# Matrix product in Winograd form on one core: in the first region of a row group, T1 of B's blocks goes ahead of the quarter sums of S4, and three of those sums move into the room of S2

## The chip, the cores and the metric

The kernel runs on one core of a Trainium2 chip. The metric is device microseconds (us) of one execution, the median of several. TensorE (PE) multiplies, VectorE (DVE) makes sums and adds results up, ScalarE (ACT) copies PSUM banks out and squares blocks, GpSimd (POOL) and SyncE (SP) issue transfers (ACT issues a few too).

## The reference

```
x = np.matmul(a, b)                    # a, b: 4096 x 4096 float32
return np.where(x > 0, x, alpha * x)   # alpha = 0.01
```

The kernel computes it in float16 blocks by Winograd's form of Strassen's scheme (seven block products in place of eight). On the way it squares A and B and takes the sums' extremes, and a branch at the end falls back to a plain bfloat16 product when the inputs are too uneven. That fallback is not taken here.

## The kernel before

**Regions.** The output is cut into regions of 1024 x 1024. A region is a pair (g, j): row group g of four, column block j of four. After the first region, which is computed while the inputs arrive, the program walks through `regions`, one group after the other. In a region A has the blocks A11, A12, A21, A22 and B has B11, B12, B21, B22, where each block is 512 columns (or rows of the output) wide and 2048 deep, in two tiles k = 0, 1 of 1024.

**Products.** `PRODUCTS` (L652) lists the seven: A11 B11, A12 B21, S2 T2, S3 T3, S1 T1, A22 T4, S4 B22. `product(n, ...)` (L792) issues number n: 64 matmuls of 128x512 at L801. The sums of A are made once for a group (`sum_a`, L566). The sums of B are made in every region, in place, by `b_sum` (L586, seen in the profile as L588): T3 into the room of B12, T2 into the room of B11, T4 into the room of B21, and T1 = B22 - T2 over T2, in the room of B11. T1 therefore has to wait until product 2 (S2 T2) has read T2, and product 4 (S1 T1) has to wait for T1.

**Quarters.** In the regions of groups 1 to 3 other than the last of groups 1 and 2, products 5 (A22 T4) and 6 (S4 B22) are themselves done by the same scheme on quarters: `sixth_in_quarters` (L843) and `seventh_in_quarters` (L892), seven `quarter_product`s of 16 matmuls of 128x256 each (L751). These need the quarter sums of A22 and of S4, four tiles each of 128x2048 float16 (512 KB). `sums_of_a` (L692) makes them: `make` takes a room, does one DVE sum (L700) and has SP store the result to DRAM (L701: `kept_qs` for S4's, `kept_qa` for A22's), from where the later regions of the group load them again (L743). This happens in the first region of each of the groups 1, 2 and 3, which the trace shows from about 412, 787 and 1160 us. Those three regions are what the change touches.

**Rooms.** S4's four sums and three of A22's four come from `new_a16()` (L762), a pool of three tiles of 512 KB, handed out in turn. So S4's fourth sum takes the tile of S4's first and has to wait until that one's store has landed; A22's first three wait for the stores of S4's second, third and fourth. The fourth of A22 lies in `t[:, 3]`. `t` (L1100) is a tile of four such rooms that is allocated right after product 2, in the room that S2 leaves. Its first three rooms serve from L1134 on for the quarter sums of B, which `sums_of_b` (L681; L686, L688, L690) makes for the sixth product.

**Order.** The order on each engine is the order of the program text. On DVE, in the first region of a group: T3 and T2 (only in group 1; the others load them), S3 and S4, the adds of product 1 to the kept sum (L967) and its leaky form (L312), T4 (L588), S4's quarter sums (L700), T1 (L588), A22's quarter sums (L700), then `t3_of_b` and `sums_of_b` (L680 to L690), the sum of two kept results (`add_v`, L972), and the adds that empty the banks of the fifth and the sixth product (L967, L856).

On PE in the same region: products 0 to 4, then the sixth product's quarter products in this order, where each names what it needs or which bank it fills: A22's (0,0) into bank one; sum 1 of A22 times sum 1 of B into bank other; (0,1) into the fourth bank; sum 2 times sum 2 onto one; sum 4 onto other; sum 3 onto one; (1,1) into the third. A bank is used again only after DVE's L856 has read it.

POOL issues the next region's blocks of B (L532, two transfers of 512 KB for each tile) whenever a product has read the old ones. SP's queue carries the output stores (L978), the copy of S4's quarter (1, 0) to DRAM (L716) and the stores of L701.

Of the kernel before, what the change touches and what calls it, by code (L numbers as in the profile page):

```python
# [47 lines left out]
def kernel(  # L48
# [402 lines left out]
    for i in range(1, len(steps)):  # L451
        t, h, u, first, last = steps[i]
# [19 lines left out]
        t, h, u, first, last = steps[i]  # L472
# [202 lines left out]
    def quarters_of_a(g, name):  # L675
        return {(h, k): operand(g, name, k)[:, :, h * HALF:(h + 1) * HALF, :] for h in range(2) for k in range(2)}
# [15 lines left out]
    def sums_of_a(g, name, room):  # L692

        x = {key: q.rearrange("p c m e -> p c (m e)") for key, q in quarters_of_a(g, name).items()}
        made = {}

        def make(n, x0, x1, op):
            made[n] = room(n)
            f = lambda t: made[t].rearrange("p (c m) -> p c m", m=2 * HALF) if isinstance(t, int) else x[t]
            nc.vector.tensor_tensor(f(n), f(x0), f(x1), op)  # L700
            nc.sync.dma_start(kept_q[name][n - 1], made[n])  # L701

        make(1, (1, 0), (1, 1), ADD)
        make(2, 1, (0, 0), SUB)
        make(3, (0, 0), (1, 0), SUB)
        make(4, (0, 1), 2, SUB)

    def x21(g, name):
        return operand(g, name, 0)[:, :, HALF:, :]

    def by_chunk(t):
        return t.rearrange("p c m e -> p c (m e)") if len(t.shape) == 4 else t.rearrange("p (c m) -> p c m", m=2 * HALF)

    def keep_x21(g, name):
        if g < G - 1:
            nc.sync.dma_start(by_chunk(kept_x21[name]), by_chunk(x21(g, name)))  # L716
# [45 lines left out]
    def new_a16(_=None):  # L762
        return a16_pool.tile([P, QUARTER], DT, name="q16", tag="a16")
# [18 lines left out]
    for i, (g, j) in enumerate(regions):  # L782
# [210 lines left out]
        def fetch_a(h, half, n):  # L993
            if n == 0:
                coming["rows", h, half] = small_pool.tile([P, 16], FP32, name="rows", tag=f"rows{half}")
            coming[h, half][n][0]()
# [21 lines left out]
        first_of_group = i == 0 or regions[i - 1][0] != g  # L1018
# [17 lines left out]
        if have_t2:  # L1036
            for k in ks:
                t = have_b[i, k, 0] = b_pool.tile([P, KC, NT], DT, name="b", tag="b11")
# [46 lines left out]
        if turning and g:  # L1085
            t3_of_b(quarters_of_b(i, 0, 1))
            for n in range(3):
                fetch_a(0, 1, n)
        if first_of_group and g:
            keep_x21(g, "s4")  # L1090
            sums_of_a(g, "s4", new_a16)
        if not g:
            bring_a(0, 1)

# [4 lines left out]
        if g:  # L1099
            t = x_pool.tile([P, 4, QUARTER], DT, name="q", tag="x")  # L1100
# [9 lines left out]
        if late_ones:  # L1110
            late_ones[0].end()
        if in_quarters and first_of_group:
            sq = {4: t[:, 3]}
            sums_of_a(g, "a22", lambda n: sq.setdefault(n, sq[4] if n == 4 else new_a16()))
            keep_x21(g, "a22")
# [106 lines left out]
    with tc.If(even == 0):  # L1222
        for m in range(M // RM):
            a_blocks = []
            for u in range(KU):
                t = a_pool.tile([P, KC // 2, RM, 2], BF16, name="a", tag=f"a{u // 2 + 1}{m % 2 + 1}")
# [6 lines left out]
            for n in range(N // NT):  # L1233
                banks = [new_bank(n % 2 * 4 + mt) for mt in range(MT)]
                cols = slice(n * NT, (n + 1) * NT)
                for u in range(KU):
                    t = b_pool.tile([P, KC, NT], BF16, name="b", tag=f"b{u // 2 + 1}{n % 2 + 1}")
# [8 lines left out]
                for mt in range(MT):  # L1246
                    t = c_pool.tile([P, 2, NT], FP32, name="c", tag=f"c{side}")[:, 0]
# [44 lines left out]
```

## Time and profile before

| what | value |
|---|---|
| median of 3 runs | 1536.24 us (1536.0 to 1539.86) |
| profiled execution | 1538.0 us |
| its span, first to last instruction | 1535.8 us |
| granted TensorE clock | 0.999 |
| PE busy, matmuls | 1523.6 us, 99% |
| DVE busy | 1158.6 us, 75% |
| ACT busy | 426.2 us, 28% |
| POOL busy | 281.8 us, 18% |
| B's blocks by POOL (q0) | 129.00 MB in all, 52.7% of 16 DMA engines' span |
| SP's transfers (q1) | 186.81 MB, 33.1% |

PE is busy nearly without a break and at full clock, so a change of the time has to appear as idle time of PE that comes or goes. The DMA share of the page's second section is in its upper tenths for most of the span: transfers share the DMA engines with many others, and how long one takes depends on what else is under way.

### The profile page before, as it was taken

Reading aid. Unit: us, or ns where it says so; the run is one execution under the profiler, and the core shown is the slowest. Engines: PE = TensorE matmul, PEld = TensorE weight load, DVE = VectorE, ACT = ScalarE, POOL = GpSimd, SP = SyncE. Lnnn points to the kernel's source line nnn. Section 1 sums busy time; section 2 is a strip of 40 time slices with the busy share of each in tenths; the row PEclk is TensorE's granted clock in tenths of the full one; section 3 lists DMA queues with packets and bytes.
Section 4 is the critical chain, followed back from the end, with each engine's and each line's share of the span. In section 5 each row is a group of like instructions: output and inputs, shape, how many; then the busy total and the mean of one; then the engine's idle time right before and its main releaser. Section 6 shows DMA issues by size and latency. Waiting matters only on the chain. (4 is left out here: it accounts for less than half of the span.)

```text
span 1535.8 us, 21827 instructions
## 1 busy us (share of the span) xinstructions
PE 1523.6 (99%) x8667; PEld 846.6 (55%) x8667; DVE 1158.6 (75%) x1207; ACT 426.2 (28%) x730; POOL 281.8 (18%) x458
## 2 busy tenths in 40 slices
PE   9999999999999999999999999999999999999998
PEld 4444444444445567574544747557554475746656
DVE  4368867765698686768769798686976968788497
ACT  2201344646310312103551031312464103041220
POOL 5641110143202011022220201110331110101100
PEclk9999999999999999999999999999999999999999
DMA  9999895998879979599798989959899895948934
GB/s 243 186 215 205 235 279 172 180 194 174 226 281 276 259 171 273 135 290 263 163 269 276 289 190 204 277 148 327 169 231 286 238 280 143 275 169 193 279 128 140
DMA packets 205442, 342.87 MB, mean 223 GB/s; under 512 B 18833, under 2 KB 148113, under 8 KB 195346
## 3 DMA queue, kind: packets, MB, share of 16 engines
q0 software_dynamic: 136704, 129.00, 52.7%
q1 hardware_dynamic: 62002, 186.81, 33.1%
q10 hardware_dynamic: 6624, 25.56, 4.4%
q8 instruction: 70, 1.15, 0.3%
q14 instruction: 42, 0.34, 0.1%
HBM read 361.76 MB, written 106.43 MB: 305 GB/s over the span
## 5 line engine op out<-in xcount | busy, mean ns | idle before, releaser
L801 PE MATMUL ps<-b,a 128*128 128x512 f16 x2624 | 570.9, 379 | 0.1
L801 PE MATMUL ps<-b,s 128*128 128x512 f16 x2240 | 489.2, 379 | 1.0 <-ACT c L814 1.0
L801 PEld LDWEIGHTS <-a 128*128 128x128 f16 x2624 | 256.8, 98 | 308.1 <-issue 0.6
L801 PEld LDWEIGHTS <-s 128*128 128x128 f16 x2240 | 219.0, 98 | 263.8 <-DVE b L588 1.5
L588 DVE TENSOR_TENSOR b<-b 128x4096 f16<-128x4096 f16 x104 | 235.1, 2289 | 66.7 <-DMA b<-in_b_dram 62.1
L532 POOL DMA_DIRECT2D b<-in_b_dram x160 | 118.5, 746 | 862.2 <-PE ps L751 325.2
L814 ACT COPY c<-ps 128x512 f32<-128x512 f32 x164 | 84.6, 596 | 444.9 <-PE ps L801 401.1
L141 DVE STREAM_TRANSPOSE a<-a 128x512 uint32<-128x512 uint32 (+2 forms) x120 | 127.0, 1106 | 101.4 <-DMA a<-in_a_dram 101.2
L132 POOL DMA_DIRECT2D a<-in_a_dram x252 | 137.3, 551 | 267.9 <-ACT junk L607 101.4
L751 PEld LDWEIGHTS <-q 128*128 128x128 f16 x1424 | 139.3, 98 | 17.8 <-issue 1.7
L607 ACT ACTIVATE junk<-a 128x512 bf16<-128x512 f16 x192 | 121.1, 631 | 99.6 <-DMA a<-in_a_dram 94.4
L312 DVE SCALAR_TENSOR_TENSOR c<-c 128x1024 f32<-128x1024 f32 (+2 forms) x123 | 141.8, 1195 | 3.9 <-ACT c L814 3.7
L230 ACT ACTIVATE sq<-b 128x2048 bf16<-128x2048 f16 x64 | 119.2, 1910 | 59.5 <-DVE sq L239 42.0
L751 PEld LDWEIGHTS <-a 128*128 128x128 f16 x1200 | 117.3, 98 | 18.7 <-DVE q L690 1.1
L967 DVE TENSOR_TENSOR c<-ps,c 128x512 f32<-128x512 f32 x140 | 87.5, 683 | 43.6 <-PE ps L801 42.0
L282 PE MATMUL ps<-b,a 128*128 128x512 f16 x512 | 112.4, 379 | 0.7 <-ACT a L379 0.2
L751 PE MATMUL ps<-b,q 128*128 128x256 f16 x784 | 91.9, 273 | 1.0 <-DVE c L856 1.0
L751 PE MATMUL ps<-b,a 128*128 128x256 f16 x752 | 88.3, 273 | 0.0
L282 PEld LDWEIGHTS <-a 128*128 128x128 f16 x512 | 49.6, 98 | 61.3 <-issue 1.7
L903 ACT COPY c<-ps 128x512 f32<-128x512 f32 x9 | 5.3, 586 | 272.0 <-PE ps L751 120.2
L751 PEld LDWEIGHTS <-s 128*128 128x128 f16 x624 | 61.1, 98 | 7.1
L856 DVE TENSOR_TENSOR c<-ps,c 128x512 f32<-128x512 f32 x80 | 52.3, 686 | 13.7 <-PE ps L751 13.7
(104 smaller groups left out, 903.7 us busy)
## 6 DMA issues: line engine op xcount, KB each, us to landing
b<-in_b_dram POOLq DMA_DIRECT2D x168, 512.0 KB, 13.9
out_dram<-c SPq DMA_DIRECT2D x240, 256.0 KB, 5.8
a<-in_a_dram POOLq DMA_DIRECT2D x244, 128.0 KB, 5.7
b<-kept SPq DMA_DIRECT2D x20, 1024.0 KB, 9.3
q<-kept_qs ACTq DMA_DIRECT2D x40, 512.0 KB, 7.9
s<-kept_s SPq DMA_DIRECT2D x18, 1024.0 KB, 7.4
q<-kept_qa SPq DMA_DIRECT2D x28, 512.0 KB, 7.5
b<-kept_last SPq DMA_DIRECT2D x12, 1024.0 KB, 11.5
```

Of the source, the lines that this page charges most:

```text
L132: nc.gpsimd.dma_start(a16[32 * q:32 * q + 32], src.rearrange("(g i) w -> i g w", i=32))
L141: nc.vector.transpose(part.rearrange("p c m e -> p c (m e)").bitcast(U32) .rearrange("p c (g i) -> p g c i", i=32), src[:, :, i * n:(i + 1 ...
L230: nc.scalar.activation(to, self.parts[n], SQUARE)
L282: nc.tensor.matmul(ps, a_cols(at[0, h, u], c, mt, (h, u) == (0, 0)), bt[0, u, nt][:, c, :], start=first, stop=last,)
L312: nc.vector.scalar_tensor_tensor(t, t, alpha, t, op0=MULT, op1=MAX if alpha <= 1 else MIN)
L532: nc.gpsimd.dma_start(t[:, c:c + 4, :], b_rows(j, u, c, 4, nt, g > 0))
L588: nc.vector.tensor_tensor(f(to), f(x0), f(x1), op)
L607: nc.scalar.activation(junk, piece[:, q, :], SQUARE, accum_out=to[:, 4 * n + q:4 * n + q + 1])
L751: nc.tensor.matmul(to[m], xq[:, c // 2, rows, c % 2], yq[:, c, :], start=first and c == 0 and m < banks, stop=c == KC - 1, skip_group_chec ...
L801: nc.tensor.matmul(banks[mt], a_cols(t, c, mt, t is first_a), B(half, nt, k)[:, c, :], start=first and (k, c) == todo[0], stop=(k, c) == t ...
L814: nc.scalar.copy(kept[mt], banks[mt])
L967: nc.vector.tensor_add(to, bank, to)
```

## The change

S4's quarter sums, with the copy of S4's quarter ahead of them, move from before product 2 to after T1, just ahead of A22's quarter sums. Three of the four no longer take a tile of the pool of three but `t[:, 0]`, `t[:, 1]` and `t[:, 2]`; the fourth takes a pool tile.

```
-        if first_of_group and g:
-            keep_x21(g, "s4")
-            sums_of_a(g, "s4", new_a16)
         if not g:
             bring_a(0, 1)
 
         product(2, y, False)
...
         if g:
             t = x_pool.tile([P, 4, QUARTER], DT, name="q", tag="x")
...
         for k in ks:
             b_sum(B(0, 0, k), B(1, 1, k), B(0, 0, k), SUB)
...
         if in_quarters and first_of_group:
+            keep_x21(g, "s4")
+            sums_of_a(g, "s4", lambda n: t[:, n - 1] if n < 4 else new_a16())
             sq = {4: t[:, 3]}
             sums_of_a(g, "a22", lambda n: sq.setdefault(n, sq[4] if n == 4 else new_a16()))
             keep_x21(g, "a22")
```

No instruction is added or removed. On DVE the two sums of T1 and the four of S4 change places; the order on PE, ACT, POOL and SP is the same as before. The waits change: T1 no longer stands behind the store of S4's first sum; S4's sums wait for S2's room (product 2 done, and S2's own copy to DRAM landed); of A22's sums only the third waits for a store of S4's, that of the fourth sum; and the three quarter sums of B wait for the stores of S4's first, third and second sum, whose rooms they take.

More of the change, by code (lines that the diff above doesn't have):

```diff
@@ L1088 @@
                 fetch_a(0, 1, n)
-        if first_of_group and g:
-            keep_x21(g, "s4")
-            sums_of_a(g, "s4", new_a16)
         if not g:
@@ L1112 @@
         if in_quarters and first_of_group:
+            keep_x21(g, "s4")
+            sums_of_a(g, "s4", lambda n: t[:, n - 1] if n < 4 else new_a16())
             sq = {4: t[:, 3]}
```

## The prediction

> **What bounds the kernel now.** I read the page first, then PE's waits, then the timelines of DVE and PE in the first regions of groups 1, 2 and 3, then the DMA view in short windows there.
>
> ```profile
> PE 1523.6 (99%) x8667; PEld 846.6 (55%) x8667; DVE 1158.6 (75%) x1207; ACT 426.2 (28%) x730; POOL 281.8 (18%) x458
> ...
> PE ps L751 <- DVE c L856: 1.3, 2, 1.0
> PE ps L801 <- ACT c L814: 1.0, 1, 1.0
> ```
>
> The first line is the page's busy row, the others are PE's waits over the whole span (total us, times, longest). PE is the wall, and the two lower lines are the only waits in the places that the change touches. All three stops lie in group 1:
>
> ```profile
> 453.01 13.98 PE L801 MATMUL ps<-b,a 128*128 128x512 f16 x64
> 467.99 13.99 PE L801 MATMUL ps<-b,s 128*128 128x512 f16 x64 [0.99 <-ACT c L814]
> ...
> 487.57 1.91 PE L751 MATMUL ps<-q,q 128*128 128x256 f16 x16 [0.36 <-DVE c L856]
> 489.36 1.91 PE L751 MATMUL ps<-b,q 128*128 128x256 f16 x16
> 492.23 1.91 PE L751 MATMUL ps<-b,q 128*128 128x256 f16 x16 [0.96 <-DVE c L856]
> ```
>
> Product 4 starts at 467.99. The page names ACT, but DVE shows the cause: the first T1 sum starts at 465.64 and one takes 2.29.
>
> ```profile
> 459.43 1.23 DVE L700 TENSOR_TENSOR q<-s 128x2048 f16<-128x2048 f16 x1
> ...
> 464.50 1.23 DVE L700 TENSOR_TENSOR q<-s,q 128x2048 f16<-128x2048 f16 x1 [1.45 <-DMA kept_qs<-q]
> 465.64 4.49 DVE L588 TENSOR_TENSOR b<-b 128x4096 f16<-128x4096 f16 x2
> 471.14 1.23 DVE L700 TENSOR_TENSOR q<-a,a 128x2048 f16<-128x2048 f16 x1 [1.01 <-DMA kept_qs<-q]
> 473.14 1.23 DVE L700 TENSOR_TENSOR q<-q,a 128x2048 f16<-128x2048 f16 x1 [0.78 <-DMA kept_qs<-q]
> 475.17 1.22 DVE L700 TENSOR_TENSOR q<-a 128x2048 f16<-128x2048 f16 x1 [0.80 <-DMA kept_qs<-q]
> 476.31 1.22 DVE L700 TENSOR_TENSOR q<-a,q 128x2048 f16<-128x2048 f16 x1
> ```
>
> The reader is to see four waits for stores of S4's sums, 4.04 us together; from 465.64 to 502 DVE has no other idle time, and PE's stops at 487.57 and 492.23 are the same lateness passed on. In groups 2 and 3 there is nothing to win: T1 is done at 840.7 and 1213.6, product 4 starts unhindered at 842.17 and 1215.18, and the only store waits are 0.37 and 0.42.
>
> **The change, part by part.**
>
> *T1 earlier.* It now follows T4: 459.43 instead of 465.64. Product 2, whose reads it has to wait for, ended about 453.0, so nothing holds it. Product 4 then starts when product 3 lets it, a product's pitch (13.82) after 453.01, at 466.83 and not 467.99: 1.16 us. In groups 2 and 3 T1 moves 5.1 us forward (to 831.12 and 1203.87, behind product 2's ends at 828.4 and 1201.4) and gains nothing.
>
> *S4's sums later.* At the spacing of before (1.26, 1.14, 1.14) they start 4.40 after T1's start: the first at 463.83, 835.52, 1208.27, the fourth at 467.37, 839.06, 1211.81. Each is stored when done, so the fourth store is issued 1.25 later, at 468.62, 840.31, 1213.06. S2's room is free: its copies were issued by 434.3, 814.7 and 1188.4, and the longest landing of such a transfer is 14.7. SP keeps its order, nothing but the stores of A22's sums stands behind these, and the output stores come some 20 us later.
>
> *The new wait.* A22's first and second sum find free pool tiles. The third, at X, takes the tile of S4's fourth sum and waits for its store; unhindered it would come 7.08 after the first S4 sum, at 470.91, 842.60, 1215.35. Behind it DVE's queue holds A22's fourth sum, the four sums of B for the sixth product, add_v, and the adds that free the banks. The three sums of B take the rooms of S4's first to third, whose stores were issued earlier and land before the fourth, so they add nothing.
>
> *What X costs.* In group 1 the third sum of A22 started at 475.17 and PE's last hindered quarter product (sum 3 onto bank one) at 492.23, with DVE unbroken between: 17.06 later. Unhindered, that product starts 8.74 after product 4's end (five quarter products at 1.747). So PE reaches it at the later of X + 17.06 and that:
> - group 2: product 4 ends 855.99, so 864.73; loss begins at X = 847.67 (before: 843.05)
> - group 3: 1228.99, so 1237.73; loss begins at 1220.67 (before: 1215.88)
> - group 1: change = X - 475.17, and at best 480.65 + 8.74 = 489.39, that is -2.84
>
> The whole change hangs on when three stores land: they may take 6.6, 7.4 and 7.6 us from issue.
>
> *The landing.* Between 833 and 837, with B's loads not yet moving, the stores took 2.6 to 2.9. From below, then, X needs no more than 2.7 us. Beside B's loads it is otherwise; these rows are of group 1, the DMA view of 462:463, 463:464, 464.2:467.2 and 468:473:
>
> ```profile
> kept_qs<-q SPq DMA_DIRECT2D x1, 512.0 KB, 9.1
> ...
> kept_qs<-q SPq DMA_DIRECT2D x1, 512.0 KB, 10.0
> ...
> q0 software_dynamic: 426, 0.43, 109.7%
> ...
> q1 hardware_dynamic: 340, 1.26, 67.1%
> q0 software_dynamic: 356, 0.36, 42.9%
> ```
>
> POOL issued a pair of B loads at 460.38 and 461.12. S4's second and third store, issued at 461.94 and 463.08, took 9.1 and 10.0. From 464.2 to 467.2 only q0 (B) moves and q1 (SP) has no packet at all; then both share, q1 at 1.26 MB in 5 us, 2.1 us for a store. Counted from the pair's first issue, the held stores land at +10.7, +12.7 and (by DVE's release at 475.17) +14.8.
>
> The same happens to the moved stores, since the next pairs are issued at 835.73 and 1208.73, just ahead of S4's first store in its new place. Before, they came behind three of the four. I take the +14.8 for the fourth, the nearest case: X = 850.5 and 1223.5, a loss of **2.8 each**. In group 1 one store more stands in the line (the first went through at once before; now it is issued at 465.1, inside the hold): 475.17 + 2.0 = 477.1, a loss of **1.9**. Ends: from below 2.7 after issue (-2.8, 0, 0); from above 14.1, the longest landing of such a store here (the copy of A22's quarter issued at 845.80): 482.7, 854.4, 1227.2, or +7.5, +6.7, +6.5.
>
> *Cover that thins.* The next region first reads a tile of B11 whose second half was issued at 483.00 and landed at 508.59; it is needed by about 509.7. The bytes are the same but move later; as PE is late too in the forecast, this costs nothing, and it would eat part of a gain.
>
> **Sum.** 1.9 + 2.8 + 2.8 = +7.5 on the span of 1535.8 (the profiled execution took 1538.0, 1.8 above the median). A difference, it goes onto the median: 1536.2 + 7.5 = **1543.7**.
>
> **Rivals.**
> 1. *Fair sharing.* SP's stores advance beside B's from 1 us after issue, at 2.1 each; the fourth lands about 1 + 8.4 + 0.5 after the first's issue (465.1, 836.8, 1209.5): 475.0, 846.7, 1219.4. All at or under the points of loss: 0, so 1536.2, not slower. The even sharing from 468 to 473 speaks for it, the empty 464.2 to 467.2 against it. The Trainium skill, "DMA: Bandwidth & Descriptors", section "Queues, rings and completion order", says that each DMA engine goes round-robin between the queues, packet by packet; by that rule the time is this rival's, and the trace agrees with it only in part of the stretch. Chance 0.21.
> 2. *Stores land alone* (2.7 after issue, as at 833 to 837): group 1 regains its 2.8, 1533.4. B's loads are under way in all three places, which speaks against it. The same page, section "Anatomy of one DMA", fits 2.0 us plus bytes at 436 GB/s, an estimate of 3.2 us for 512 KB, which would mean this case; the 9.1 and 10.0 disagree. Chance 0.05.
> 3. *Held twice.* All four stores wait out the pair, or the next pair (467.29, 842.64, 1215.64) holds the last again: A22's stores in these slots landed at 478.5, 855.7 (the fourth) and 1228.2. X of 479, 855.7, 1226.5 gives 3.8 + 8.0 + 5.8 = 17.6, 1553.8. Chance 0.16.
>
> **How the numbers follow.** Forecast 0.58 (its own range 1541 to 1548). A measurement tells about 0.3%, 4.6 us, from no change. PE's idle time in these places is 2.8, so faster by more is left at 0.01 for scatter; same 0.25 (rivals 1 and 2); slower 0.74 (forecast and rival 3). The range reaches from rival 1 into rival 3: 1535.5 to 1552.
>
> **What would show it.** T1 at about 459.4, 831.1, 1203.9 and no stop ahead of product 4. One long DVE wait at L700 for kept_qs in each region, 6 to 9 us, where four short ones stood. PE stops at L751 behind L690 or L856 in all three regions, 2 to 3 us together in each. Fourth stores of kept_qs that land 8.5 to 11 us after issue. Wrong: landings under 7 us, or a DVE wait ahead of L686 instead.

## The result, and the profile after

The changed kernel takes 1542.67 us (median of 15 runs, 1540.94 to 1547.26), the kernel before 1536.0 us (15 runs, 1533.49 to 1541.61). The ratio is 1.0049, 95% interval 1.0041 to 1.0057: 6.7 us slower. The forecast was 7.5 us slower. The profiled execution of the changed kernel took 1542.67, its span is 1540.7.

DVE's timeline in the first region of group 1, after the change:

```profile
453.58 8.89 DVE L588 TENSOR_TENSOR b<-b 128x4096 f16<-128x4096 f16 x4
462.38 1.23 DVE L700 TENSOR_TENSOR q<-s 128x2048 f16<-128x2048 f16 x1
...
468.31 1.23 DVE L700 TENSOR_TENSOR q<-q,a 128x2048 f16<-128x2048 f16 x1
475.87 1.22 DVE L700 TENSOR_TENSOR q<-a 128x2048 f16<-128x2048 f16 x1 [6.33 <-DMA kept_qs<-q]
```

T4 and T1 now stand in one row (four sums), S4's sums behind them, and where four waits for stores stood there is one, at A22's third sum. It is the same in groups 2 and 3; this is the view of DVE's waits over the whole span (total us, times, longest):

```profile
DVE q L700 <- DMA kept_qs<-q: 21.1, 3, 7.6
```

Three waits, 6.33, 7.17 and 7.58. PE in group 1, after:

```profile
452.76 13.98 PE L801 MATMUL ps<-b,a 128*128 128x512 f16 x64
466.58 13.98 PE L801 MATMUL ps<-b,s 128*128 128x512 f16 x64
480.39 1.91 PE L751 MATMUL ps<-b,a 128*128 128x256 f16 x16
483.07 1.92 PE L751 MATMUL ps<-q,q 128*128 128x256 f16 x16 [0.77 <-DVE q L690]
484.83 1.91 PE L751 MATMUL ps<-b,a 128*128 128x256 f16 x16
488.27 1.91 PE L751 MATMUL ps<-q,q 128*128 128x256 f16 x16 [1.53 <-DVE c L856]
490.06 1.91 PE L751 MATMUL ps<-b,q 128*128 128x256 f16 x16
492.93 1.91 PE L751 MATMUL ps<-b,q 128*128 128x256 f16 x16 [0.96 <-DVE c L856]
```

Product 4 follows product 3 without a stop, 13.82 behind it: the gain is there, 1.16 us. The sixth product's quarter products then stop three times. From product 3's start to the last stopped quarter product it was 492.23 - 453.01 = 39.22 and is 492.93 - 452.76 = 40.17: group 1 loses 0.95 on balance.

Since no matmul was added, removed or moved, the two traces can be laid over one another: the same matmul's start, after less before, changes wherever PE stops more or less. This gives the whole account. The second column sets a second execution of both kernels (`before_again`, `after_again`, below, taken on two different chips) against each other.

| where PE's start moves | first profiles, us | second profiles, us |
|---|---|---|
| group 1, product 4 no longer waits for T1 | -1.17 | -0.50 |
| group 1, sixth product in quarters | +2.12 | +2.06 |
| group 2, sixth product | +0.32 | +1.36 |
| group 3, sixth product | +0.88 | +0.20 |
| group 2, the *next* region | +0.75 | +0.85 |
| group 3, the *next* region | +1.38 | +2.64 |
| sum | +4.28 | +6.61 |
| span | 1535.8 to 1540.7, +4.9 | 1533.5 to 1540.5, +7.0 |

What is left in the first column is the start of the program, -0.25, a piece of -0.40 at 1174 us, and 1.3 after the last matmul; in the second -0.10, -0.08 and 0.5 at the same places. So there are two losses of about the same size: the one that was forecast, in the first regions, and one behind them that the prediction had put at nothing. PE's timeline and DVE's in group 3's second region, after the change, show the second:

```profile
1301.53 1.92 PE L751 MATMUL ps<-b,q 128*128 128x256 f16 x16 [0.73 <-DVE q L734]
...
1308.21 1.92 PE L751 MATMUL ps<-q,a 128*128 128x256 f16 x16 [1.26 <-DVE q L690]
```

```profile
1276.44 2.29 DVE L588 TENSOR_TENSOR b<-b 128x4096 f16<-128x4096 f16 x1 [13.44 <-DMA b<-in_b_dram]
...
1281.49 4.69 DVE L588 TENSOR_TENSOR b<-b 128x4096 f16<-128x4096 f16 x2 [0.37 <-DMA b<-in_b_dram]
```

The same rows before:

```profile
1298.38 1.91 PE L751 MATMUL ps<-b,q 128*128 128x256 f16 x16
...
1304.56 1.92 PE L751 MATMUL ps<-q,a 128*128 128x256 f16 x16 [0.78 <-DVE q L690]
```

```profile
1272.79 2.29 DVE L588 TENSOR_TENSOR b<-b 128x4096 f16<-128x4096 f16 x1 [12.05 <-DMA b<-in_b_dram]
...
1277.84 4.69 DVE L588 TENSOR_TENSOR b<-b 128x4096 f16<-128x4096 f16 x2 [0.37 <-DMA b<-in_b_dram]
```

DVE waits there for the last loads of the next B before it can make T3 and T2: the first of the two DVE rows is for one tile, the second for the other. The very last load landed at 1277.72 before and lands at 1281.37 after, 3.65 later, where PE had been made only 2.26 late until then. DVE has nothing to make this up with, and 1.38 arrives at PE 20 to 27 us on.

### The profile page after: what moved, and what is told of

It is laid out like the page before. It is cut to its first block, busy times and chain, and to the rows that moved or that the text cites. A ratio compares the mean times of both kernels' runs of the same rounds, so it can differ in the third digit from the quotient of the medians.

```text
span 1540.7 us, 21831 instructions
## 1 busy us (share of the span) xinstructions
PE 1525.1 (99%) x8667; PEld 846.8 (55%) x8667; DVE 1157.4 (75%) x1207; ACT 426.4 (28%) x730; POOL 282.0 (18%) x458
## 5 line engine op out<-in xcount | busy, mean ns | idle before, releaser
L801 PE MATMUL ps<-b,a 128*128 128x512 f16 x2624 | 570.7, 379 | 0.0
L801 PE MATMUL ps<-b,s 128*128 128x512 f16 x2240 | 489.2, 379 | 0.5 <-DVE b L588 0.5
L801 PEld LDWEIGHTS <-a 128*128 128x128 f16 x2624 | 256.7, 98 | 307.9 <-issue 0.3
L801 PEld LDWEIGHTS <-s 128*128 128x128 f16 x2240 | 219.1, 98 | 263.1 <-issue 1.0
```

Of the source, the lines that this page charges most:

```text
L801: nc.tensor.matmul(banks[mt], a_cols(t, c, mt, t is first_a), B(half, nt, k)[:, c, :], start=first and (k, c) == todo[0], stop=(k, c) == t ...
```

## The experiments

In all of them the theory is: the change costs what its later stores cost, once by the wait of A22's third sum and once by the bytes, which leave a quiet stretch and make B's loads for the next region late. Times of "before" beside each are from the same chip.

**1. New rooms, old order.** S4's sums ahead of T1, still in S2's room:

```
+        if in_quarters and first_of_group:
+            keep_x21(g, "s4")
+            sums_of_a(g, "s4", lambda n: t[:, n - 1] if n < 4 else new_a16())
         for k in ks:
             b_sum(B(0, 0, k), B(1, 1, k), B(0, 0, k), SUB)
...
-            keep_x21(g, "s4")
-            sums_of_a(g, "s4", lambda n: t[:, n - 1] if n < 4 else new_a16())
```

> S4's quarter sums lie in S2's room as in the change, but are made ahead of T1 again, right behind T4. Theory (the change costs what S4's later stores cost: the third sum of A22 waits for the fourth store, held behind B's loads, and the stores' bytes move into a busy stretch, so that B lands later for the next region): the stores are issued as early as in the kernel before, the fourth lands by about 842 in group 2 and 1215 in group 3, no stop of PE in the first regions of groups 2 and 3; T1 still ends before product 3 does, so group 1 keeps the 1.2 us; 1534 to 1536. Rival (the rooms are to blame: one tile of the pool for the fourth sum and S2's room for the others make a wait that was not there): nearly all of the loss stays, 1541 to 1543.

Measured: 1534.04 us (11 runs), before 1534.87; ratio 0.9994, 0.9985 to 1.0003. The whole loss is gone with the order, and the rooms by themselves cost nothing. In groups 2 and 3 the four stores were issued at 826.68 to 830.21 and 1200.44 to 1203.97, ahead of B's pairs at 832.05 and 1204.65, and landed within 3.03. DMA view of 826:832 in a second execution of this version (`new_rooms_again`):

```profile
kept_qs<-q SPq DMA_DIRECT2D x4, 512.0 KB, 2.8
```

and PE's waits over its whole span:

```profile
PE turned L372 <- DVE a_rounded L356: 1.4, 1, 1.4
PE wp L105 <- DVE x L91: 1.2, 1, 1.2
PE ps L282 <- ACT a L379: 0.2, 1, 0.2
```

These are the start of the program; after it PE does not stop at all.

**2. T1 ahead, old rooms.** The converse: the change's order, all four sums from the pool (`new_a16` in place of the lambda).

> T1 goes ahead of S4's quarter sums as in the change, but all four of these take tiles of the pool of three, as before. Theory: the same late stores, and the chain of waits of before on top: in group 1 the fourth S4 sum waits for the first store (about 471), is itself stored after that, and the third of A22 waits for it until about 480, 4 us later than in the change; in groups 2 and 3 the first store lands before it is needed, so these are as in the change; 1545 to 1548. Rival (the rooms are to blame): the loss goes with the rooms, 1535 to 1538.

Measured: 1545.99 (6 runs), before 1534.87; 1.0070, 1.0054 to 1.0086. As the theory said, and the rival falls. Group 1's DVE shows the chain that the old rooms make of late stores:

```profile
469.57 1.22 DVE L700 TENSOR_TENSOR q<-s,q 128x2048 f16<-128x2048 f16 x1 [5.24 <-DMA kept_qs<-q]
471.42 1.23 DVE L700 TENSOR_TENSOR q<-a,a 128x2048 f16<-128x2048 f16 x1 [0.63 <-DMA kept_qs<-q]
473.13 1.23 DVE L700 TENSOR_TENSOR q<-q,a 128x2048 f16<-128x2048 f16 x1 [0.48 <-DMA kept_qs<-q]
477.07 1.23 DVE L700 TENSOR_TENSOR q<-a 128x2048 f16<-128x2048 f16 x1 [2.72 <-DMA kept_qs<-q]
```

It differs in the place: group 1 came out about 3 us better than expected (A22's third sum at 477.07, not 480), while group 3, where the fourth sum itself waited 4.65, lost 2.7 more than in the first profile of the change.

**3. Half of T1 ahead.** Only the first tile of T1 stands ahead of S4's sums.

```
         for k in ks:
             b_sum(B(0, 0, k), B(1, 1, k), B(0, 0, k), SUB)
+            if in_quarters and first_of_group and k == ks[0]:
+                keep_x21(g, "s4")
+                sums_of_a(g, "s4", lambda n: t[:, n - 1] if n < 4 else new_a16())
```

> As the change, but only the first tile of T1 goes ahead of S4's sums, the second follows them: the stores come 2.2 us earlier than in the change, 2.2 later than in the kernel with the old order and the new rooms. Theory: most of the hold is avoided, the fourth store is issued within a us of B's pair in groups 2 and 3 and lands after about 5 us, no direct stop; one store moves into the busy stretch, not three; group 1 keeps the 1.2 us: 1535 to 1538, between the two. A rival by which the cost goes with T1's place alone gives half of the loss, 1539.

Measured: 1537.96 (12 runs), before 1534.87; 1.0019, 1.0010 to 1.0028. Between the two, near the theory's upper end. The mixture is plain in the trace: group 2's fourth store was issued at 835.01, 0.12 behind the pair's first load, and landed after 3.69, no stop; group 3's at 1210.52, 2.37 behind it, and landed after 10.56, a stop of 1.03. Group 1 is like group 3: three stores issued 1.42 to 3.7 behind the pair's first load, a wait of 6.13 at A22's third sum, and stops, where none was expected. The time of the stores against B's pair decides, not T1's place: in both regions T1's first tile had moved alike. The program text alone does not fix this time: DVE arrives up to 3 us earlier or later against PE from one execution to the next.

**4. B's pair later.** The change, with the next region's B11 loaded ahead of its B12 in these three regions, so that no load is under way at the stores.

> The changed kernel, but in the first regions of groups 1 to 3 POOL issues the next region's B11 ahead of its B12, so that no load of B is under way when S4's sums are stored, and every load comes some 14 us later. Theory (the stores are held by B's loads): the stores land 2.6 to 3 us after issue, A22's third sum waits for nothing or under 1 us, and the first regions have no stop; the next regions wait for B, 5 us or more each: 1550 or more. Rival (the stores are slow by themselves, four in a row from one queue): they land after 7 us or more here too.

Measured: 1556.72 (one run, so without an interval), before 1534.62. DMA view of 836:840:

```profile
kept_qs<-q SPq DMA_DIRECT2D x4, 512.0 KB, 2.7
```

and all of DVE's waits for these stores over the span, 3.6 us where the change has 21.1:

```profile
DVE q L700 <- DMA kept_qs<-q: 3.6, 3, 2.2
```

So the stores are not slow by themselves. B's loads hold them, and without these the first regions lose nothing. (In group 3 the last two stores took 4.4 and 4.6 and A22's third sum waited 2.24, more than expected, but PE did not stop there either.) The price comes in the next regions, which wait for B: PE's waits there are 16.4 us together. Some 4.6 more come from the clock. The granted TensorE clock was 0.5 for 6.83 us from 914.28 and for 3.41 us from 1296.57, each time with a stop of PE (4.4 and 3.6 us), so idle time is not the whole price of a long stop.

**5. Fewer stores.** In groups 2 and 3 only S4's fourth sum is stored. This kernel leaves out three stores in each of them, and the later regions there load group 1's sums in their place, so it no longer computes the product; it serves only to show where the time goes.

```
-            nc.sync.dma_start(kept_q[name][n - 1], made[n])
+            if name != "s4" or g == 1 or n == 4:
+                nc.sync.dma_start(kept_q[name][n - 1], made[n])
```

> The changed kernel, but in groups 2 and 3 the first three sums of S4 are not stored (later regions of these groups load the sums of group 1 in their place); the fourth store stays where it is. Theory: the fourth store no longer has three others ahead of it but still meets B's pair: it lands 5 to 8.5 us after issue, in place of 9.5 to 9.9; no direct stop in groups 2 and 3, and as 1.5 MB less move in the busy stretch there, the later stops in these groups go too; only group 1's loss of about 1 is left: 1535 to 1538. If the place in line were everything, the fourth store would land in 2.7; if the bytes did not matter, the stops in the second regions would stay and the time be 1540.

Measured: 1539.24 (6 runs), before 1534.62; 1.0033, 1.0021 to 1.0045. Above the expected range, and the trace says why: groups 2 and 3 lose nothing, neither in the first regions nor in the next (against `before_again`, PE's start moves by 2.9 up to the end of group 1's first region, and by 0.34 in all that follows), but group 1, which was left as it is, loses 3.2 here and not 1: its fourth store was issued 1.01 behind the first load of the *next* pair and took 9.17, and the kernel before has less of its own stops in this profile than in the first. DMA view of 838:841, the fourth store of group 2:

```profile
kept_qs<-q SPq DMA_DIRECT2D x1, 512.0 KB, 7.4
```

Alone in its line it still takes 7.4 (7.35 in group 3): the hold by B's pair is most of the delay, the three stores ahead of it the rest, 2.1 and 2.6 us (9.52 and 9.92 in the change). With 1.5 MB less in each of these stretches the late B loads are gone too.

**6. The fourth store first.** All four stores are issued after the last sum, in the order 4, 1, 2, 3.

```
+            if name != "s4":
                 nc.sync.dma_start(kept_q[name][n - 1], made[n])
...
+        if name == "s4":
+            for n in (4, 1, 2, 3):
+                nc.sync.dma_start(kept_q[name][n - 1], made[n])
```

> The changed kernel, but SP issues the four stores of S4's sums together after the last sum, the fourth store first. Theory: it no longer stands behind three others; held only by B's pair it lands about 5 to 8 us after issue, 2 to 4 us earlier than in the change, so that the direct stops in groups 2 and 3 go and group 1 gains 2 to 3; the bytes still move in the busy stretch, so the later landing of B in the next region stays: 1538 to 1540. If the wait at the third sum of A22 were all of the loss, 1534 to 1536; if the place in the line told nothing, 1542 to 1543.

Measured: 1549.82 (6 runs), before 1534.87; 1.0087, 1.0073 to 1.0102. None of the three expected times. The half about the wait held in part: the fourth stores took 3.17, 7.66 and 8.73, A22's third sum waits 0.82 in group 1, where PE gains 2.6 on the first profile of before, and group 2's first region has no stop; but the sum still waits 5.32 and 6.38 in groups 2 and 3, and group 3 stops for 0.6. Three stores now all move after B's pair, and PE's waits name what follows:

```profile
PE ps L805 <- DMA b<-in_b_dram: 9.0, 3, 4.2
PE ps L755 <- DVE q L738: 2.1, 1, 2.1
```

(L805 is L801 of the other kernels, shifted by the added lines.) Its PE timeline at the start of group 1's second region:

```profile
504.72 1.89 PE L805 MATMUL ps<-b,a 128*128 128x512 f16 x8
510.82 1.44 PE L805 MATMUL ps<-b,a 128*128 128x512 f16 x3 [4.21 <-DMA b<-in_b_dram]
```

Product 0 of the next region stands still after eight matmuls, until the second half of its B11 tile lands (510.78). This is the thin cover that the prediction had named, with its condition fulfilled: PE was not late, so the late load shows. At the start of group 2's second region product 0 stands twice more, 1.4 and 3.3 us.

The stops do not add up to the loss, because the clock adds to them. With the stop at 510.82 the granted TensorE clock was 0.5 for 6.83 us (from 509.26) and with the later ones for 3.41 us (from 891.55): the matmuls of 128x512 then start 0.43 us apart and not 0.22, which costs PE some 2.5 and 1.7 us more. In the changed kernel the clock has no such stretch before the last matmul.

**7. Rooms in turn.** Stores as in the change; A22's third sum takes the room of S4's first, B's last quarter sum the tile of S4's fourth, and the sums that are loaded for the next region (`following`) go into rooms that fit this.

```
...
+            spare = new_a16()
-            sums_of_a(g, "s4", lambda n: t[:, n - 1] if n < 4 else new_a16())
-            sq = {4: t[:, 3]}
+            sums_of_a(g, "s4", lambda n: t[:, n - 1] if n < 4 else spare)
+            sq = {4: t[:, 3], 3: t[:, 0]}
...
+            tq = {2: t[:, 1], 4: t[:, 2], 1: spare} if first_of_group else {2: t[:, 0], 1: t[:, 1], 4: t[:, 2]}
```

> The changed kernel with its stores at the same times and in the same order, but the rooms handed on in another turn: A22's third sum takes the room of S4's first sum (whose store lands first), and B's last quarter sum the tile of S4's fourth. Nothing waits for the fourth store until 4.7 us later in DVE's order. Theory: no stop ahead of the sixth product's quarter products in groups 2 and 3, and group 1 gains its 2.8; but the stores still move in the busy stretch, and since PE is no longer late itself, the next regions now wait for B's loads, as when the fourth store went first: 1540 to 1548, with stops at the start of the second regions of the groups. Rival (the direct wait is all of the loss, the later B loads are a matter of chance): 1533 to 1536.

Measured: 1540.67 (5 runs), before 1534.62; 1.0041, 1.0027 to 1.0055. This separates the two losses. The stops in the first regions are gone, group 1 regains its 2.0, and yet nearly the whole loss is still there. PE's waits:

```profile
PE ps L751 <- DVE q L734: 2.1, 1, 2.1
PE ps L801 <- DMA b<-in_b_dram: 2.1, 3, 1.1
PE ps L751 <- DVE q L690: 1.3, 1, 1.3
```

All of these lie in second regions. The two losses do not simply add: it looks as if a PE that is made late by the first hides part of the second.

**8. Both kernels again.**

> The kernel before once more, for a second profile of it: 1533 to 1537. Theory: the same four short waits for S4's stores; the stops of PE in group 1 depend on how early DVE gets there and may differ by 1 to 2 us from the first profile, which took 1538.

> The changed kernel once more, on the chip of the next three runs: 1.004 to 1.006 of the kernel before, 1540 to 1543. Theory: third sums of A22 that wait 5 to 8 us, 2 to 4 us of stops in the first regions together, and 1 to 3 us in the second regions of groups 2 and 3.

Measured: before 1535.72 (one run); after 1542.85 (5 runs) against 1534.04, 1.0058, 1.0044 to 1.0072. The table above has their account. The stops of PE in group 1 of the kernel before were 2.3 in its first profile and 1.5 in the second.

**9. Is there something to gain?** Three runs on one chip, before at 1534.04: experiment 1 again; experiment 1 with the rooms of experiment 7; experiment 1 with S4's sums ahead of T4 too.

> The version with the old order and the new rooms once more, for a tighter interval: 0.998 to 1.000 of the kernel before, 1532 to 1535. Theory: it has the two halves of the gain that the profile of before allows (T1 in time for product 4, fewer store waits), 1.5 to 2.9 us in group 1 and nothing elsewhere.

> The old order with the rooms handed on in the other turn: no sum of A22 or B waits for a store that has not landed. Theory: the store waits were already off PE's path in the old order with the new rooms (one wait of about 1 us in group 1), so this gives the same time, 1532 to 1535; a rival by which any wait of DVE in this place costs PE gives 1 us less.

> New rooms, and S4's sums as early as their room allows: ahead of T4 as well, which then comes between them and T1. The stores go 4.4 us earlier in group 1 and up to 3 us earlier in groups 2 and 3, where DVE now waits for product 2 to end. Theory (the stores' bytes count by where they move): all stores of S4 are through before B's loads start, and A22's too go out as before; no stop in the three groups, 1532 to 1534.5. Rival: T4 and T1 end too close to product 4 and it waits again, 1535 to 1536.

Measured: 1533.6 (0.9998, 0.9989 to 1.0007), 1534.01 (1.0002, 0.9993 to 1.0011) and 1534.97 (1.0004, 0.9995 to 1.0013), 11 runs each. None differs measurably from the kernel before; the third lies a little above its expected range. PE's own stretches show the gain in all three, 2.0 us in group 1 against `before_again`, but the medians do not. Either the profiled executions of the kernel before have more of these stops than its usual ones, or something after the last matmul takes the gain back. The record leans to the first: both profiled executions of the kernel before were above the median of their kernel, by 2.0 us (1538.0 for 1536.0) and 1.1 (1535.72 for 1534.62), while the stretch behind the last matmul is only 0.4 to 0.6 longer in the three than in `before_again`. It is not shown, and stays open.

## Why the prediction was right, and where it was not

The sign, the size (7.5 for 6.7) and the cause in outline were right: later stores, held by B's loads. The sum inside was not.

- **T1 earlier, 1.16 us in group 1 and nothing elsewhere.** Right: 1.17 in the trace, and no T1 stop in groups 2 and 3 in any run. In the second pair of profiles it is 0.50, since T1 was less late there.
- **What X costs.** Right, nearly to the hundredth. X is 475.87, 848.68 and 1222.92 in the trace after. PE's start at these places, ahead of the loss itself, had moved by -0.25, +0.70 and +1.38; set back by that, X is 476.12, 847.98, 1221.54, and the formula gives 476.12 - 475.17 = 0.95, 847.98 - 847.67 = 0.31, 1221.54 - 1220.67 = 0.87. The trace has 0.95, 0.32, 0.88. In the second profile, set back in the same way, X is 849.02 and 1220.85 in groups 2 and 3, which gives 1.35 and 0.18; the trace has 1.36 and 0.20.
- **The landing.** This term was mis-sized: X was put at 477.1, 850.5 and 1223.5 and is 476.1, 848.0, 1221.5, so that 1.9 + 2.8 + 2.8 became 0.95 + 0.32 + 0.88. The prediction carried over the +14.8 of a fourth store that stood third among *held* ones. In groups 2 and 3 the first two stores got through before or at the start of the hold (they took 2.63 and 5.13 in group 2, 2.68 and 5.13 in group 3), and only two were held, so that these took 8.55 to 9.92 and X came 12.2 and 12.8 after the pair's first load. DVE had also come to S4's sums 1.2 to 1.9 us earlier, measured against PE, than the first profile of before let expect. With 2 us more or less in X, the loss in groups 2 and 3 is all or nothing, which is why the second profile has 1.36 and 0.20 there.
- **"As PE is late too in the forecast, this costs nothing"** (the cover that thins). This step failed. The prediction looked at one load, B11's tile that the next region reads first, in group 1, and there it holds in the change: the load lands at 507.14 and is needed at about 510.4. In group 2 it does not hold even for that tile: its second half lands at 883.31, and the matmul that reads it starts at 883.35, 0.16 late (0.45 in the second profile). And the other loads of the next B land later too, by the bytes of the stores that now move among them; the last ones are read by DVE (T3 and T2) and by ACT's squares (in group 2, where ACT waits 0.65 for such a load), each with nothing to spare. The kernel before shows this lack of slack: the stop of 0.78 at 1304.56 above is in its list of PE's waits. The term put at nothing costs 2.13 in the first profiles and 3.49 in the second, about as much as the forecast's own term (2.15 and 3.12). Experiments 6 and 7 show that it grows when PE is less late, experiment 5 that it goes with the bytes.
- **Rival 1, fair sharing,** falls: X, set back, came 1.1 to 2.1 us behind the points of that rival (475.0, 846.7, 1219.4), and the fourth store alone in its line took 7.4. The round-robin between queues by the Trainium skill, "DMA: Bandwidth & Descriptors", section "Queues, rings and completion order", is seen while both queues have packets on the way (468 to 473 in the trace of before: 340 packets of SP's queue beside 356 of POOL's); it does not tell of the microseconds until the stores' packets begin to move. Experiment 4 shows that B's loads cause these; by which part of the DMA engines, no run here shows.
- **Rival 2, stores that land alone,** is the state of groups 2 and 3 in experiment 1 and of groups 1 and 2 in experiment 4: 2.6 to 3.0 us. The estimate of 3.2 us beside it rests on a fit that the Trainium skill, "DMA: Bandwidth & Descriptors", section "Anatomy of one DMA", gives for transfers issued by GpSimd, and these stores are SP's.
- **Rival 3, held twice,** did not come about: the next pair was issued after all four stores in groups 2 and 3; in group 1 the next load was issued at 467.04, 0.12 ahead of the fourth store, and X still came at 475.87. Its price has one term without a row: with the landing of 1228.2 that it names, group 3 would lose 7.5 and not 5.8.
- **The signs.** The one long wait of DVE in each region came (6.33, 7.17, 7.58, for 6 to 9), and the fourth stores of groups 2 and 3 took 9.52 and 9.92 (for 8.5 to 11). PE's stops in the first regions were 3.26, 0.16 and 0.72, not 2 to 3 in each.

The total was right because a term that was too large by 5.4 (7.5 for 2.15 in the first profiles) stood beside one of 2.1 to 3.5 that was missing, with the executions' own scatter for the rest. That 7.5 came so near to 6.7 is luck.

## What to carry to other kernels

Count a moved step's transfers by *when* they move: in groups 2 and 3 the change moved 1.5 MB of stores by 2 to 3 us (first profiles), out of a stretch in which the DMA engines had nothing else to do and into one in which loads fill them, and that decided. A transfer that goes later delays not only who waits for it but everything that is queued beside it, and the one who pays may be the next stage: follow the loads that share the stretch to their last reader. And where a loss begins at a point (X = 847.7), say by how much the arrival scatters before taking a single value for it.

## What the runs showed of the hardware that was not expected

A store of 512 KB from SP lands in 2.6 to 3.0 us in most places where no load of POOL's (float32 to float16, 512 KB written) is under way or about to begin; in a few it took 4.2 to 4.7 (group 1 of experiments 1 and 9, group 3 of experiment 4), and why, no run here shows. Issued 1 to 5 us after the first of a pair of these loads, it took 5.3 to 13.2 over all the runs. In group 3 of experiment 3 the store issued 0.10 us behind that first load took 3.48, and the next one, 1.23 us behind it, 9.59: a microsecond in the order of issue was worth 6 in the landing.

The granted clock was halved, to 0.5, for 3.41 or 6.83 us with some stops of PE of 2.15 to 4.4 us (experiments 2, 4, 5 and 6), and stayed at 1.0 with others of 2.15 (experiment 7) and 3.54 (experiment 4, at 537 us). Behind the stops in second regions (experiments 4 and 6) this cost PE 1.7 to 2.9 us more than the stop; behind those in group 1's first region (experiments 2 and 5) it cost nothing more, since PE then had to wait for DVE in any case. What decides whether it happens, no run here shows.
